# Seven block products instead of eight for three of eight pairs in an output projection

## The chip, the core and the metric

The kernel runs on one core of one Trainium2 chip. The metric is the device time of one execution in microseconds (us), median over runs. Five engines run their own instruction queues in order: PE (TensorE, matmuls), DVE (VectorE), ACT (ScalarE), POOL (GpSimd) and SP (SyncE, which here only issues transfers). They meet through semaphores. The profile names weight loads of PE apart, as PEld.

## The reference

Two layers of an encoder, 256 positions, width 2048, all in float32. Layer 0 mixes tokens with a gated MLP, layer 1 with latent attention (16 heads); each mixer and each feed-forward block ends in a residual sum and a layer norm. What the change touches is the last line of the attention and the norm behind it:

```
o = chunk_causal_attention(q_nope, q_rope, k_nope, k_rope, v)      # (1, 256, 16 heads, 128)
m = o.reshape(B, S, MLA_HEADS * V_DIM) @ w_out                     # (256 x 2048) @ (2048 x 2048)
x = layer_norm(ALPHA * x + m, ln_mix_g[i], ln_mix_b[i])
f = conv_ffn(x, ffn_w_up[i], ffn_conv_w[i], ffn_conv_b[i], ffn_w_down[i])
```

## The kernel before

**Float32 by parts.** Every float32 matrix is split into a rounded part (`wh`, made on ACT with a copy) and the rest (`wl`, made on DVE as raw minus rounded). One block product is then three matmuls of 512 columns: high by high, low by high, high by low (`prod_b`, line 366; every matmul is recorded at line 230, in `mm`).

**Weights.** A `Feed` walks one list of chunks, 1 MB each. SP loads a chunk into one of 3 `raw` buffers, ACT and DVE split it, PE uses it. The split parts stand in a pool with the tag `big`: 14 slots of 1 MB. A slot is given again when the last reader of its old content is done, so an ACT or DVE instruction that writes into a slot can wait for PE.

**The attention's output projection.** The 2048 columns of the result are done in two halves. For the first half (accumulators `mo0`) the matmuls are woven between the scores and the products of the heads. The second half (`mo1`) is a loop over eight chunks; a chunk is a pair of row blocks k (128 rows each) by 1024 columns. For each pair there are eight block products: two row blocks by two halves of positions (b) by two column blocks of 512 (f). The last three pairs (`SKEW`) are kept in `late`. `end_mo` adds them accumulator by accumulator, so that the accumulators finish one after the other, and `boundary` weaves the norm between: `piece` (add to the residual, statistics), `start` (mean and root), `scale` (normalize on DVE), `put` (four transposes on PE into `lnt`, scale and shift on ACT into `lny`, then the split into `xhl`, high part on ACT, low part on DVE). The first products of the feed-forward block (`upf`) read `xhl`.

**Seven products.** In the other large products of the kernel some pairs already use seven block products (Winograd's form of Strassen's method) by `Banks.seven`, `Feed._seven` and `combine`. Seven products need sums of the weights' blocks (`ts`, split into `th` and `tl`), sums of the activations' blocks (made by `turn` and `combine`), four further accumulators, and at the end `Banks.rest` and `Norm.fold`, eight DVE instructions that give back the four shared parts. A pair with eight products takes 2 slots of `big`, one with seven takes 5 (`ts`, `wh`, `wl`, `th`, `tl`).

**What sets the order.** The code is recorded by a tile framework. Its scheduler turns the recorded program into one fixed order per engine, by priorities and its own estimates of durations, with the needed semaphores. Lines such as `order(...)` and `keep_in_program_order` pin a few of them. On the chip each engine takes its instructions strictly in that order.

**Slots around the change.** During `mo1` the pool `big` holds `oT` (the heads' results, 4 slots) and the residual `res` (2 slots) throughout.

Of the kernel before, what the change touches and what calls it, by code (L numbers as in the profile page):

```python
# [8 lines left out]
F32 = mybir.dt.float32  # L9
F32R = mybir.dt.float32r  # L10
BF16 = mybir.dt.bfloat16
AF = mybir.ActivationFunctionType
ALU = mybir.AluOpType
AX = mybir.AxisListType

P = 128
S = 256
# [7 lines left out]
H = 16  # L25
# [19 lines left out]
SKEW = 3  # L45
# [5 lines left out]

U_PAIRS = [[0, 1, 5, 7, 2, 6, 3, 4]] + [[0, 1, 2, 5, 3, 7, 4, 6]] * 5
U_SEVEN = [(2, 3)] + [(2, 3, 4)] * 4 + [(2, 3)]

T1, T2 = 6, 5
SLOTS = {"big": 14, "raw": 3, "side": 6}
# [153 lines left out]
def trunk(ctx: ExitStack, tc: tile.TileContext, x, xT, gm_in, gm_wout, ffn_up, ffn_dn,  # L210
          ml_q, ml_kv, ml_b, ml_out, consts, w_sT, b_s, ropes, ln_rows, out):
    nc = tc.nc
# [3 lines left out]
    tp = ctx.enter_context(tc.tile_pool(name="tp", bufs=3))  # L216
# [6 lines left out]
    def slot(shape, name, dt=F32, tag="big"):  # L223
        return big.tile(shape, dt, tag=tag, name=name, bufs=SLOTS[tag])

    def bank(name):
        return ps.tile([P, 512], F32, tag="bank", name=name)

    def mm(o, l, r, start, stop):
        recent[0] = nc.tensor.matmul(o, l, r, start=start, stop=stop, skip_group_check=True)  # L230
        return recent[0]
# [12 lines left out]
    chunks, parked = [], []  # L244
# [4 lines left out]
    for g in range(6):  # L249
        for p in U_PAIRS[g]:  # L250
            i = 48 + 8 * g + p // 2
            w = gm_in[i : i + 5 : 4, :, p % 2 * 1024 : p % 2 * 1024 + 1024].rearrange("f p c -> p f c")
            chunks.append((w, 2048, "seven" if p in U_SEVEN[g] else "wide"))

# [15 lines left out]
    chunks += [(ml_q[i], 2048, "") for i in range(4)]  # L270
    chunks += [(ml_kv[i], 3 * KVR, "") for i in range(5)] + [(ml_kv[5, :, 0:KVR], KVR, "")]
    chunks += [(ml_b[i], 2048, "") for i in range(ml_b.shape[0])]
    chunks += [(ml_out[i], 2048, "") for i in range(ml_out.shape[0])]
    chunks += [(ffn_up[1, i], 2048, "") for i in range(n_up)]
    back(ffn_dn[1], NF_FF)

# [1 line left out]
    feed = Feed(nc, tc.keep_in_program_order, behind, order, big, dram, chunks)  # L278
# [9 lines left out]
    def turn(t, k1, k2):  # L288

        at = lambda k, b: k[:, b] if len(k.shape) == 3 else k[:, b * P : (b + 1) * P]  # L290
        tc.keep_in_program_order(nc.vector.tensor_tensor(t[:, 0], at(k1, 0), at(k1, 1), ALU.subtract))
        nc.vector.tensor_tensor(t[:, 1], at(k1, 1), at(k2, 1), ALU.subtract)
        nc.vector.tensor_tensor(t[:, 2], t[:, 1], at(k1, 0), ALU.subtract)
        nc.vector.tensor_tensor(t[:, 3], at(k2, 0), t[:, 2], ALU.add)

    def combine(name, o, k1, k2):


        t = tp.tile([P, 4, P], F32, tag="t2", name=f"xs{name}", bufs=T2)
        turn(t, k1, k2)  # L300
        o = o.rearrange("p (h s c) -> p h s c", h=2, s=4)
        nc.scalar.copy(o[:, 0], t)
        nc.vector.tensor_tensor(o[:, 1], t, o[:, 0].bitcast(F32), ALU.subtract)
        return [(o[:, 0, i], o[:, 1, i]) for i in (1, 2, 0, 3)]

    for j in range(4):
        t = slot([P, 4, S], f"xraw{j}", tag="side")
# [47 lines left out]
    def x_parts(xs, k, b):  # L355
        t = xs[k // 4]
        return (t[:, k % 4, b * P : (b + 1) * P], t[:, k % 4, S + b * P : S + (b + 1) * P])

    def prod_b(acc, parts, hi, lo, pieces, first, last):

        xh, xl = parts
        for f, (o, w) in enumerate(pieces):
            mm(acc[f][:, :w], xh, hi[:, o : o + w], first, False)
            mm(acc[f][:, :w], xl, hi[:, o : o + w], False, False)
            mm(acc[f][:, :w], xh, lo[:, o : o + w], False, last)
# [37 lines left out]
    OWN, DIRECT = ("p1", "q5", "p7", "p6"), ("q3", "p2", "e", "q4")  # L403
# [327 lines left out]
    halfp = [(0, 512), (512, 512)]  # L731
# [19 lines left out]
    for gi in range(6):  # L751

        acc = Banks(f"v{gi}", DIRECT if gi == 0 else OWN + DIRECT if gi % 2 else DIRECT + OWN)
        rest = (None,) * 4
        for c, p in enumerate(V_PAIRS[gi]):
            a = [[x_parts(xhl, 2 * p + j, b) for j in range(2)] for b in range(2)]
            got = feed.next()
# [19 lines left out]
            if c == 7 and gi == 5:  # L777
                wTg = []
                for i in range(4):
                    t = tp.tile([P, 2, P], F32, tag="t1", name=f"wT{i}", bufs=T1)  # L780
# [72 lines left out]
    def turned(g, tiles):  # L853

        for i, t in enumerate(tiles):
            src = v[g][:, i // 2, i % 2 * 512 : i % 2 * 512 + 512]
            for j in range(4):
                nc.tensor.transpose(t[:, j * P : (j + 1) * P], src[:, j * P : (j + 1) * P], ident)
            nc.scalar.copy(src, t)
# [7 lines left out]
    for g in range(6):  # L867
        direct, own = (ub[4:], ub[:4]) if g % 2 else (ub[:4], ub[4:])
        acc = Banks(f"u{g}", DIRECT + OWN, direct + own)
        for c, p in enumerate(U_PAIRS[g]):  # L870
            a = [[x_parts(xhl, 2 * p + j, b) for j in range(2)] for b in range(2)]
            got = feed.next()
            if p in U_SEVEN[g]:
                acc.seven(a, xc[p], *got, turned=512, across=True)
                if p == U_SEVEN[g][-1]:
                    rest = acc.rest()
# [21 lines left out]
    ln = Norm(0, {})  # L898
    acc, end = down(NF_GM, pT, "wo", ln, acts, tiles=ub, beside=lambda: turned(5, ub[4:]))
# [66 lines left out]
    ln, acc, end = ffn(0, ln, acc, end, False)  # L966
# [61 lines left out]
    acc = [[bank(f"mkv{b}_{f}") for f in range(2)] for b in range(2)]  # L1028
    for c in range(6):
        hi, lo = feed.next()  # L1030
        for j in range(3 if c < 5 else 1):
            k = 3 * c + j
# [9 lines left out]
    for b in range(2):  # L1042
# [3 lines left out]
        t = tp.tile([P, 4, ROPE], F32, tag="t1", name=f"kr2_{b}", bufs=T1)  # L1046
# [18 lines left out]
    acc = [[bank(f"qr{b}_{f}") for f in range(2)] for b in range(2)]  # L1065
    for c in range(2):
        hi, lo = feed.next()
        for j in range(2):
            k = 2 * c + j
# [52 lines left out]
    oT = []  # L1122
# [41 lines left out]
    def attend_b(h):  # L1164

        p = probs[h]
        pt = bank(f"pt{h}")
        for j in range(3):
            nc.tensor.transpose(pt[:, j * P : (j + 1) * P], p[:, j * P : (j + 1) * P], ident)  # L1169
        pts = tp.tile([P, 3 * P], F32, tag="t2", name=f"pts{h}", bufs=T2)  # L1170
        nc.scalar.copy(pts, pt[:, : 3 * P])
        probs[h] = pts

    def attend_c(h):
        if h % 4 == 0:
            oT.append(slot([P, 4, 512], f"oT{h // 4}", F32R))
        pts = probs.pop(h)
        o = bank(f"o{h}")
        c = slice(h * P, (h + 1) * P)
        mm(o[:, 0:S], vv[0][:, c], pts[:, 0:S], True, False)  # L1180
        mm(o[:, P:S], vv[1][:, c], pts[:, S : 3 * P], False, True)
        hi = oT[h // 4][:, h % 4, 0:S]
        nc.scalar.copy(hi, o[:, 0:S])
        nc.vector.tensor_tensor(oT[h // 4][:, h % 4, S : 2 * S], o[:, 0:S], hi.bitcast(F32), ALU.subtract)

    for hf in range(2):
        acc = [[bank(f"vv{hf}_{b}_{f}") for f in range(2)] for b in range(2)]
        for c in range(2):
            hi, lo = feed.next()
            for j in range(2):  # L1190

                k = 2 * c + j
# [7 lines left out]
        for b in range(2):  # L1200
            for f in range(2):
                c = slice(hf * 1024 + f * 512, hf * 1024 + (f + 1) * 512)
# [3 lines left out]
    ln = Norm(2, res)  # L1206
    acc = [[bank(f"mo0_{b}_{f}") for f in range(2)] for b in range(2)]
    LAG = 4
    attend_c(0)
    for t in range(3, H + LAG):  # L1210
        k = t - LAG
        if k >= 0:
            if k % 2 == 0:
                hi, lo = feed.next()
            w = slice((k % 2) * 1024, (k % 2) * 1024 + 1024)
        if 3 < t < H:
            attend_a(t)
        if k >= 0:
            prod_b(acc[0], x_parts(oT, k, 0), hi[:, w], lo[:, w], halfp, k == 0, k == KD - 1)
        if t < H + 2:  # L1220
            attend_c(t - 2)
        if k >= 0:
            prod_b(acc[1][:1], x_parts(oT, k, 1), hi[:, w], lo[:, w], halfp[:1], k == 0, k == KD - 1)
        if t - 1 < H:
            attend_b(t - 1)
        if k >= 0:
            prod_b(acc[1][1:], x_parts(oT, k, 1), hi[:, w], lo[:, w], halfp[1:], k == 0, k == KD - 1)
    ln.begin()
    ln.prep()
    for b in range(2):  # L1230
        for f in range(2):
            ln.piece(b, f, acc[b][f])
    acc = [[bank(f"mo1_{b}_{f}") for f in range(2)] for b in range(2)]
    late = []
    for c in range(8):
        left = 7 - c
        hi, lo = feed.next(splits=2 if left > 5 else 3, loads=2)
        for j in range(2):
            k = 2 * c + j
            w = slice(j * 1024, (j + 1) * 1024)  # L1240
            if left < SKEW:
                late.append((hi[:, w], lo[:, w], k))
                continue
            for b in range(2):
                prod_b(acc[b], x_parts(oT, k, b), hi[:, w], lo[:, w], halfp, k == 0, False)

    def end_mo(b, f):
        for hi, lo, k in late:
# [3 lines left out]
    ln, acc, end = ffn(1, ln, banks, end_mo, True)  # L1252
# [99 lines left out]
```

## Time and profile before

| what | value |
|---|---|
| time, median of 3 runs | 2465.73 us (2465.49 to 2466.3) |
| span of the profiled execution, first to last instruction | 2464.6 us |
| PE busy in the span | 2458.1 us, granted clock 1.000 |
| DVE busy | 2054.7 us |
| ACT busy | 1459.3 us |
| matmuls into `mo`, both halves: first and last start | 1637.3 and 1749.9 us |
| first product of the feed-forward block behind them, on PE | 1750.6 us |

The profiled execution has a span and no separate time of its own; the runs' times are whole device times, and their median lies 1.1 us over the span. Times of places below are us from the span's start. A busy PE in the profile is one with a matmul in its pipeline. Names lose their buffer numbers in the profile: `mo` is every accumulator of this projection.

### The profile page before, as it was taken

How to read it: one execution, taken by the hardware profiler on the slowest of the kernel's cores; microseconds unless marked ns; L12 is line 12 of the kernel's file. 1: busy time of each engine (PE TensorE's matmuls, PEld its weight loads, DVE VectorE, ACT ScalarE, POOL GpSimd, SP SyncE). 2: the span in 40 equal slices, each digit the busy share in tenths (PEclk: the TensorE clock that was granted, in tenths of full speed). 3: DMA queues.
4: the chain of work that ended last, by engine and by line, in shares of the span. 5: the costliest groups of instructions: out<-in, count | busy, mean ns of one | idle time of the engine just before them, and what ended most of it. 6: DMA issues, size and time to landing. Idle time of an engine off the chain costs nothing. (4 is left out here: it accounts for less than half of the span.)

```text
span 2464.6 us, 32483 instructions
## 1 busy us (share of the span) xinstructions
PE 2458.1 (100%) x12494; PEld 2091.3 (85%) x12494; DVE 2054.7 (83%) x2734; ACT 1459.3 (59%) x1967; POOL 104.2 (4%) x202
## 2 busy tenths in 40 slices
PE   9999999999999999999999999999999999999999
PEld 7888888888888888888888888988888888888887
DVE  7999999989897788778777997867598787878798
ACT  6666665566565666656554566665565665555453
POOL 0000000000000000000001000000000000000000
PEclk9999999999999999999999999999999999999999
DMA  7555666656665778778868885544478787777885
GB/s 291 202 208 205 226 204 202 205 188 205 222 212 198 241 282 314 300 279 300 322 218 318 301 301 182 184 170 156 172 269 309 275 305 304 295 265 278 299 324 201
DMA packets 116428, 611.94 MB, mean 248 GB/s; under 512 B 10648, under 2 KB 10912, under 8 KB 75184
## 3 DMA queue, kind: packets, MB, share of 16 engines
q1 hardware_dynamic: 90128, 462.47, 52.9%
q0 software_dynamic: 26144, 147.39, 15.8%
q8 instruction: 98, 1.61, 0.3%
q14 instruction: 58, 0.48, 0.1%
HBM read 544.75 MB, written 65.06 MB: 247 GB/s over the span
## 5 line engine op out<-in xcount | busy, mean ns | idle before, releaser
L128 DVE TENSOR_TENSOR wl<-raw,wh 128x1024 fp32r<-128x1024 f32 (+4 forms) x645 | 958.4, 1501 | 169.5 <-ACT wh L125 124.0
L125 ACT CAST wh<-raw 128x1024 fp32r<-128x1024 f32 (+4 forms) x645 | 809.0, 1278 | 356.8 <-PE up L230 80.7
L230 PE MATMUL up<-xhl,wh 128*128 128x512 f32 x2624 | 611.4, 390 | 0.0
L230 PEld LDWEIGHTS up<-xhl,wh 128*128 128x128 f32 x2624 | 487.4, 188 | 97.8
L230 PEld LDWEIGHTS up<-xhl,wl 128*128 128x128 f32 x2624 | 325.8, 192 | 6.4
L230 PE MATMUL up<-xhl,wl 128*128 128x256 f32 x2624 | 328.1, 283 | 0.0
L125 ACT CAST th<-ts 128x1536 fp32r<-128x1536 f32 (+1 forms) x138 | 142.5, 1052 | 110.9 <-DVE ts L135 80.3
L230 PE MATMUL ub<-wh,xhl 128*128 128x512 f32 x576 | 179.5, 393 | 0.0
L128 DVE TENSOR_TENSOR tl<-ts,th 128x1536 fp32r<-128x1536 f32 (+1 forms) x138 | 163.2, 1221 | 10.4 <-PE dn_p L230 3.4
L230 PEld LDWEIGHTS ub<-wh,xhl 128*128 128x128 f32 x576 | 108.1, 188 | 24.2 <-issue 1.9
L230 PE MATMUL ub<-wl,xhl 128*128 128x512 f32 x288 | 112.1, 389 | 0.0
L135 DVE TENSOR_TENSOR ts<-ts,raw 128x512 f32<-128x512 f32 x138 | 95.1, 689 | 1.4
L135 DVE TENSOR_TENSOR ts<-raw 128x1024 f32<-128x1024 f32 x69 | 84.3, 1221 | 6.1 <-PE ub L230 3.8
L230 PE MATMUL mo<-wh,oT 128*128 128x512 f32 x256 | 82.5, 401 | 0.0
L230 PE MATMUL v_q<-wh,xhl 128*128 128x512 f32 x224 | 70.7, 391 | 0.3 <-ACT wh L125 0.3
L230 PEld LDWEIGHTS ub<-wl,xhl 128*128 128x128 f32 x288 | 54.1, 188 | 11.3
L230 PE MATMUL v_p<-wh,xhl 128*128 128x512 f32 x192 | 59.9, 389 | 0.0
L230 PEld LDWEIGHTS mo<-wh,oT 128*128 128x128 f32 x256 | 45.5, 189 | 7.1
L230 PEld LDWEIGHTS v_q<-wh,xhl 128*128 128x128 f32 x224 | 42.0, 188 | 10.5 <-ACT wh L125 1.9
L230 PE MATMUL mo<-wl,oT 128*128 128x512 f32 x128 | 50.1, 391 | 0.0
L724 ACT ACTIVATE lny<-lnt,lncol 128x128 f32<-128x128 f32 x96 | 36.6, 472 | 15.6 <-PE lnt L720 15.5
L388 DVE TENSOR_TENSOR h_0a<-up,lo_0a 128x256 f32<-128x256 f32 x41 | 17.2, 421 | 33.0 <-ACT lo_0a L386 33.0
(1838 smaller groups left out, 4338.4 us busy)
## 6 DMA issues: line engine op xcount, KB each, us to landing
raw<-in_ffn_up_dram SPq DMA_DIRECT2D x172, 1024.0 KB, 7.0
raw<-in_gm_in_dram SPq DMA_DIRECT2D x93, 1024.0 KB, 5.3
raw<-in_ffn_dn_dram SPq DMA_DIRECT2D x68, 1024.0 KB, 7.2
raw<-in_gm_wout_dram SPq DMA_DIRECT2D x48, 1024.0 KB, 5.3
praw<-in_ffn_dn_dram POOLq DMA_DIRECT2D x16, 1024.0 KB, 13.9
keptth<-pth POOLq DMA_DIRECT2D x16, 1024.0 KB, 8.1
kepttl<-ptl POOLq DMA_DIRECT2D x16, 1024.0 KB, 8.8
fth<-keptth POOLq DMA_DIRECT2D x16, 1024.0 KB, 9.4
```

The lines of the kernel that those rows point to most:

```text
L125: cast = self.nc.scalar.copy(hi, raw)
L128: self.nc.vector.tensor_tensor(lo, raw, hi.bitcast(F32), ALU.subtract)
L135: add = lambda o, a, b: self.nc.vector.tensor_tensor(o, a, b, ALU.add)
L230: recent[0] = nc.tensor.matmul(o, l, r, start=start, stop=stop, skip_group_check=True)
L388: nc.vector.tensor_tensor(h, acc[:, 0:S], lo, ALU.add)
L724: nc.scalar.activation(y[:, j], t[:, j * P : (j + 1) * P], AF.Identity, bias=lncol[:, o : o + 1], scale=lncol[:, g : g + 1])
```

## The change

Pairs 2, 3 and 4 of the eight pairs of the second half take seven block products. The sums of activations for these pairs are made on DVE and ACT (`sum_heads`) at the end of the attention, behind the last scores. They stand in two further slots of `big` (`mos`) until the projection has used them. All eight accumulators are taken from the start; behind pair 4 `rest` and `fold` add the shared parts to the residual, and the four `piece` calls at the end become plain adds.

```diff
+MO_SEVEN = (2, 3, 4)
...
-    chunks += [(ml_out[i], 2048, "") for i in range(ml_out.shape[0])]
+    chunks += [(ml_out[i], 2048, "seven" if i - 8 in MO_SEVEN else "") for i in range(ml_out.shape[0])]
...
     attend_c(0)
+    mo_sums, mo_room = {}, []
+
+    def sum_heads(c):
+
+        if len(mo_sums) % 2 == 0:
+            mo_room.append(slot([P, 2, 8 * P], f"mos{c}", F32R))
+        x = oT[c // 2][:, 2 * (c % 2) : 2 * (c % 2) + 2]
+        raw = tp.tile([P, 2, S], F32, tag="t2", name=f"mor{c}", bufs=T2)
+        nc.vector.tensor_tensor(raw, x[:, :, 0:S].bitcast(F32), x[:, :, S : 2 * S].bitcast(F32), ALU.add)
+        mo_sums[c] = combine(f"mo{c}", mo_room[-1][:, len(mo_sums) % 2, :], raw[:, 0], raw[:, 1])
+
...
             attend_b(t - 1)
+        if 0 <= t - H - 1 < len(MO_SEVEN):
+            sum_heads(MO_SEVEN[t - H - 1])
...
-    acc = [[bank(f"mo1_{b}_{f}") for f in range(2)] for b in range(2)]
+    mo = Banks("mo1", DIRECT + OWN)
+    acc = [[mo.acc[DIRECT[2 * b + f]] for f in range(2)] for b in range(2)]
     late = []
     for c in range(8):
         left = 7 - c
-        hi, lo = feed.next(splits=2 if left > 5 else 3, loads=2)
-        for j in range(2):
-            k = 2 * c + j
-            w = slice(j * 1024, (j + 1) * 1024)
-            if left < SKEW:
-                late.append((hi[:, w], lo[:, w], k))
-                continue
-            for b in range(2):
-                prod_b(acc[b], x_parts(oT, k, b), hi[:, w], lo[:, w], halfp, k == 0, False)
+        got = feed.next(splits=2 if left > 5 else 3, loads=2)
+        if left < SKEW:
+            for j in range(2):
+                w = slice(j * 1024, (j + 1) * 1024)
+                late.append((got[0][:, w], got[1][:, w], 2 * c + j))
+            continue
+        a = [[x_parts(oT, 2 * c + j, b) for j in range(2)] for b in range(2)]
+        if c in MO_SEVEN:
+            mo.seven(a, mo_sums[c], *got)
+        else:
+            mo.eight(a, *got)
+        if c == MO_SEVEN[-1]:
+            for j, t in enumerate(mo.rest()):
+                ln.fold(j // 2, 2 + j % 2, t)
```

The change also makes the scheduler write another order around the end of the projection. The first place is PE's queue there. Before, with `mo_1_1` the last accumulator to finish and `lnt_0_0` the first transposes of the norm of the first 128 positions:

```order
L230 MATMUL mo_1_0_14431<-wl_14570,oT_14275 128x512
L230 MATMUL mo_1_1_14432<-wh_14503,oT_14074 128x512
L720 MATMUL lnt_0_0_14695<-ident,res_0_10982 128x128 x4
L230 MATMUL mo_1_1_14432<-wh_14503,oT_14074 128x512
L230 MATMUL mo_1_1_14432<-wl_14504,oT_14074 128x512
L230 MATMUL mo_1_1_14432<-wh_14503,oT_14074 128x512 x2
```

After, with `mo_q_14461` the last accumulator (the same block of the result as `mo_1_1`):

```order
L232 MATMUL mo_q_14461<-wh_14620,oT_14275 128x512 x2
L232 MATMUL mo_q_14461<-wl_14621,oT_14275 128x512
L722 MATMUL lnt_0_0_14757<-ident,res_0_10982 128x128 x4
L722 MATMUL lnt_0_1_14789<-ident,res_0_10982 128x128 x4
L232 MATMUL upf_0_14804<-wh_14663,xhl_0_14753 128x512
L722 MATMUL lnt_0_2_14818<-ident,res_1_11812 128x128 x4
L232 MATMUL upf_0_14804<-wh_14663,xhl_0_14753 128x512
```

The first transposes moved from one matmul into the last accumulator's products to behind all 18 of them.

The second place is DVE's queue at the same end. Before, where `res_0` and `res_1` are the residual's two column halves and `lnmv_0` is the mean and variance of the first 128 positions:

```order
L128 TENSOR_TENSOR wl_14610<-raw_14575,wh_14609 128x1024 x2
L666 SCALAR_TENSOR_TENSOR res_1_11812<-res_1_11812,mo_0_0_14429 128x512
L667 BN_STATS lnst_0_14419<-res_1_11812 128x6
L666 SCALAR_TENSOR_TENSOR res_1_11812<-res_1_11812,mo_0_1_14430 128x512
L667 BN_STATS lnst_0_14419<-res_1_11812 128x6
L672 BN_AGGR lnmv_0_14665<-lnst_0_14419 128x2
L351 RECIPROCAL lnrs_0_14669<-lnrs_0q 128x1
L679 TENSOR_SCALAR res_0_10982<-res_0_10982,lnmv_0_14665,lnrs_0_14669 128x512 x2
L666 SCALAR_TENSOR_TENSOR res_1_11812<-res_1_11812,mo_1_0_14431 128x512
```

After, from the third of the feed-forward block's weight splits on:

```order
L130 TENSOR_TENSOR wl_14680<-raw_14669,wh_14679 128x1024 x2
L666 TENSOR_TENSOR res_1_11812<-res_1_11812,mo_q_14458 128x512
L666 TENSOR_TENSOR res_1_11812<-res_1_11812,mo_p_14459 128x512
L669 BN_STATS lnst_0_14448<-res_1_11812 128x6 x2
L666 TENSOR_TENSOR res_1_11812<-res_1_11812,mo_e 128x512
L674 BN_AGGR lnmv_0_14727<-lnst_0_14448 128x2
L666 TENSOR_TENSOR res_1_11812<-res_1_11812,mo_q_14461 128x512
L669 BN_STATS lnst_1_14449<-res_1_11812 128x6 x2
L353 RECIPROCAL lnrs_0_14731<-lnrs_0q 128x1
L674 BN_AGGR lnmv_1_14843<-lnst_1_14449 128x2
L681 TENSOR_SCALAR res_0_10982<-res_0_10982,lnmv_0_14727,lnrs_0_14731 128x512 x2
```

The add of the last accumulator and the statistics of the second 128 positions now stand ahead of the first scaling of the first 128 positions, and three instead of two pairs of the feed-forward block's weights are split ahead of all that.

## The prediction

> **What bounds the kernel now.** I read the page first, then the busy times of the stage, then the timelines of PE and DVE around it.
>
> ```profile
> PE 2458.1 (100%) x12494; PEld 2091.3 (85%) x12494; DVE 2054.7 (83%) x2734; ACT 1459.3 (59%) x1967; POOL 104.2 (4%) x202
> PE 33%; DMA 1%; DVE 1%; issue 0%; ACT 0%; DVEq 0%; ACTq 0%
> ```
>
> PE is never idle for long and heads the chain of waits, so a matmul saved is time saved, as long as nothing makes PE wait. But DVE is busy for 83% of the span, and the change takes work from PE and gives work to DVE. So what counts is DVE's room in this stage. The busy times of two stretches of the second half (stretch and length, then busy us and number of instructions of PE, PEld, DVE, ACT and POOL, then granted clock and DMA):
>
> ```profile
> 1706.10:1717.00 10.90, 10.90 (x49) 9.03 (x49) 7.79 (x10) 4.01 (x4) 0.00 (x0) 1.00 0.52 191
> 1717.00:1750.00 33.00, 33.00 (x149) 27.29 (x149) 19.51 (x24) 15.00 (x19) 0.00 (x0) 1.00 0.50 187
> ```
>
> In the last 33 us DVE works 19.5 us; it has 13.5 us of room. Next, PE's rows there (start, duration, instruction):
>
> ```profile
> 1734.72 0.62 PE L230 MATMUL mo<-wh,oT 128*128 128x512 f32 x2
> 1735.40 0.62 PE L230 MATMUL mo<-wh,oT 128*128 128x512 f32 x2
> ...
> 1745.84 0.60 PE L720 MATMUL lnt<-ident,res 128*128 128x128 f32 x4
> ...
> 1749.94 0.39 PE L230 MATMUL mo<-wl,oT 128*128 128x512 f32 x1
> 1750.17 0.60 PE L720 MATMUL lnt<-ident,res 128*128 128x128 f32 x4
> ...
> 1751.62 0.50 PE L230 MATMUL upf<-wh,xhl 128*128 128x512 f32 x1
> ```
>
> Three matmuls, one block product, start 0.68 us after the three before: 0.227 us each. From the last matmul into `mo` at 1749.94, back over 192 of them and four transposes (about 0.4 us), the second half starts at about 1706.1, and its second pair ends at 1717.0 (48 x 0.227 = 10.9). The norm's first transposes run inside the last accumulator's products, and `upf` follows without a hole. DVE's rows show why:
>
> ```profile
> 1697.50 0.54 DVE L1161 TENSOR_SCALAR p<-p,mx 128x128 f32<-128x128 f32 x2
> ...
> 1744.00 1.00 DVE L679 TENSOR_SCALAR res<-res,lnmv,lnrs 128x512 f32<-128x512 f32 x2
> ...
> 1751.48 0.68 DVE L666 SCALAR_TENSOR_TENSOR res<-res,mo 128x512 f32<-128x512 f32 x1
> ```
>
> The first row is the last head's probabilities, needed below. DVE scales the first 128 positions at 1744.0, some 6 us before PE is done, and adds the last accumulator only at 1751.5.
>
> **What is removed.** Three pairs save one block product each: 9 matmuls x 0.227 = 2.0 us of PE, 0.08% of the time. That is the whole possible gain, and it is smaller than the 0.2% (4.9 us) that a measurement of this kernel can tell from no change.
>
> **What is added, and where it lies.** On DVE, all for float32. The same steps exist in the kernel's other products; what counts is the time until the next instruction starts, which is about 0.09 us less than the duration where rows follow each other. First a pair with seven products:
>
> ```profile
> 1363.77 1.22 DVE L135 TENSOR_TENSOR ts<-raw 128x1024 f32<-128x1024 f32 x1
> ...
> 1366.71 1.75 DVE L128 TENSOR_TENSOR wl<-raw,wh 128x1536 fp32r<-128x1536 f32 x1
> 1368.38 0.69 DVE L135 TENSOR_TENSOR ts<-ts,raw 128x512 f32<-128x512 f32 x1
> 1368.98 2.36 DVE L128 TENSOR_TENSOR tl<-ts,th 128x1536 fp32r<-128x1536 f32 x2
> 1371.25 0.69 DVE L488 TENSOR_TENSOR dn018wx<-act,dn018wx 128x512 fp32r<-128x512 f32 x1
> ```
>
> Then `rest` and `fold`, eight instructions from the first row to the second:
>
> ```profile
> 1375.52 0.69 DVE L451 TENSOR_TENSOR dn00u<-dn_p,dn00p 128x512 f32<-128x512 f32 x1
> ...
> 1380.32 1.23 DVE L128 TENSOR_TENSOR wl<-raw,wh 128x1024 fp32r<-128x1024 f32 x1
> ```
>
> Then two statistics and four splits in a row, in this stage:
>
> ```profile
> 1705.61 1.28 DVE L667 BATCH_NORM_STATS2 lnst<-res 128x6 f32<-128x512 f32 x2
> ...
> 1727.95 4.63 DVE L128 TENSOR_TENSOR wl<-raw,wh 128x1024 fp32r<-128x1024 f32 x4 [3.08 <-issue]
> ```
>
> A split of 1024 columns takes (4.63 - 1.22) / 3 = 1.135 us, a sum of 512 columns 0.60 (1368.38 to 1368.98), the split of 1536 columns 1.67, `tl` 2.27 and two statistics 1.2. A seven costs DVE 1.13 + 0.60 + 1.67 + 0.60 + 2.27 = 6.27 us against 2.27 for a plain pair. PE uses it up in 21 x 0.227 = 4.8 us. Three in a row put DVE behind.
>
> *The anchor.* `big` has 14 slots; `oT` holds 4, `res` 2 and the new sums 2, which leaves 6. Pairs 0 and 1 hold 4, so the first seven gets its fifth buffer, `tl`, only when PE is done with pair 1, at 1717.0. The sums themselves (three times two instructions of 0.60 and four short ones of 0.20, 6.0 us) lie before that. Pair 1's split (2.27) now stands behind them in DVE's queue instead of ahead of the last probabilities, so these move from 1697.5 to 1695.2. From there I count 0.5 (probabilities) + 0.3 (`oT`) + 6.0 (sums) + 0.3 (`oT`) + 2.3 (split of pair 1) + 4.8 (first half's adds and statistics) + 4.0 (first seven up to `tl`) = 18.2 us, done at about 1713.4. The sums cost nothing, with 3.6 us to spare; beyond that the rest moves with them.
>
> *DVE from 1717.0 to the first scaling*, in the order that its queue has after the change: `tl` of the first seven 2.27; two more sevens 12.54; the three late pairs 6.82; `rest` and `fold` 4.80 (1375.52 to 1380.32); three pairs of the feed-forward block 6.82; four adds and four statistics, 0.60 each, 4.80; mean, root and their waits about 0.5; the first scaling 0.5. Sum 39.1 us, so the first transposes can start at 1756.1. PE's own work from 1717.0 is 63 matmuls of sevens and 72 late ones, 135 x 0.227 = 30.7 us: done at 1747.7. PE waits about 8.4 us, because the queue has the scaling behind everything else. Waits of PE for a late `th` or `wl` before that only take from those 8.4.
>
> *The restart.* What follows a set of transposes is seen later in this boundary, on PE, ACT and DVE:
>
> ```profile
> 1759.94 0.60 PE L720 MATMUL lnt<-ident,res 128*128 128x128 f32 x4
> 1760.58 1.51 ACT L724 ACTIVATE lny<-lnt,lncol 128x128 f32<-128x128 f32 x4 [1.69 <-PE lnt L720]
> 1762.12 0.62 ACT L727 CAST xhl<-lny 128x512 fp32r<-128x512 f32 x1
> 1762.77 0.69 DVE L728 TENSOR_TENSOR xhl<-lny,xhl 128x512 fp32r<-128x512 f32 x1 [2.44 <-ACT xhl L727]
> ```
>
> From transposes to the low part of `xhl` 3.5 us, plus 0.4 for a fifth `lny` that stands ahead of the cast: 3.9. DVE's other seven scalings (0.46 each) fit within it. So the second matmul of `upf`, at 1751.62 before, comes at 1756.1 + 3.9 = 1760.0: 8.4 us later. The 2.0 saved is in this already. From there PE is the bound again as before, and nothing gives the delay back.
>
> *Hidden:* ACT gets three `mos` casts, three `th` and one copy; with 15.0 of 33 us used it stays off the path. SP issues the same transfers in the same order, later by what DVE is late with `raw`. The transfers of these weights land after 4.8 us (median):
>
> ```profile
> raw<-in_ffn_up_dram SPq DMA_DIRECT2D x10, 1024.0 KB, 4.8
> ```
>
> The last pair ahead of the norm can be loaded when DVE ends the late pairs; DVE then has 4.8 + 4.5 us of other work, which leaves 4.5 us for ACT's casts. If that cover went, DVE would wait and the end would move by as much.
>
> **The clock.** A hole of 8 us in PE does not occur in the middle of this trace. What an idle PE costs is seen at both ends of the span, in PE's first and last rows and in the busy times of the last 2.6 us:
>
> ```profile
> 1.31 4.45 PE L230 MATMUL warm<-idle 128*128 128x512 bf16 x10 [1.31 <-POOL idle L281]
> ```
>
> ```profile
> 2457.51 2.84 PE L230 MATMUL fin<-lng,dg 128*128 128x512 f32 x6 [0.27 <-DVE dg L701]
> ```
>
> ```profile
> 2462.00:2464.60 2.60, 0.00 (x0) 0.00 (x0) 0.00 (x0) 0.00 (x0) 0.00 (x0) 0.82 0.26 101
> ```
>
> Ten matmuls of 512 columns took 4.45 us at the start, 0.445 each, nearly twice 0.227: half speed, 2.2 us lost before full speed. After PE's last matmul (end at 2460.35) the granted clock averages 0.82 from 2462.0 to 2464.6; if it fell to 0.5 it did so at about 2463.7, 3.3 us into the idle time. A hole of 8 us should do the same, and PE then pays the start again: 2.2 us, the nearest row, with 0 and 4.4 (twice) as ends. The Trainium skill ("TensorE: Matmul & The Clock Gate", section "Part 1: The HAM clock gate") says that PE's clock halves after an idle window of about 3.4 us and comes back after about 3.4 us of sustained work. The trace's two ends agree (3.3 us and 4.45 us). By the page alone the loss would be an estimated 1.7 to 3.4 us, and the sum 2475.8 to 2477.5 us.
>
> **Sum.** 8.4 + 2.2 = 10.6 us on the profiled span of 2464.6 us, which lies 1.1 us below the median of the runs, 2465.73: 2476.3 us, 0.43% slower.
>
> **Rivals.**
> - *The same hole, and the clock stays.* For it: no hole in mid-program shows a fall. Against: the end of the span. 2465.7 + 8.4 = 2474.1.
> - *DVE keeps up; not slower.* Against it stand 39.1 us of DVE rows in 33 us. It needs some 6 us less, as if the fifth buffer came earlier or the rows ran closer. The queue order alone would still make PE wait from 1747.7 for one add, two statistics, root and a scaling (0.7 + 1.2 + 0.3 + 0.5 = 2.7), then 3.9 us to the second `upf` matmul, at 1754.3: +2.7, 2468.4, no change by the 0.2%.
> - *Only the saved products show.* If besides that the scaling were ready in time: 2465.7 - 2.0 = 2463.7, also no change. It decides for this once DVE is done by 1744 as before; the order on DVE, which puts the last accumulator's add first, excludes it nearly.
> - *Buffers starve the sevens.* With six slots for five buffers each, the later sevens wait for slots that PE frees late, and DVE stands still in between. For it: the first seven does so. Against: DVE is behind by then and finds the slots free. One further wait of a product's four groups, 4 x 0.68 = 2.7 us, with the clock: 2479.
>
> **How the numbers follow.** Hole and clock 0.62; hole alone 0.20; buffers 0.07; DVE keeps up 0.07; saved products alone 0.04. The likeliest gives 2476.3. Its own range is 2474 to 2479, from 1.5 us on DVE's chain either way and the clock's ends cut at about their middles. The range to hold 8 in 10 is 2471.5 to 2480: below, the hole alone with DVE's chain 2.6 us shorter; above, DVE's 1.5 us and the clock's upper end together. Slower by over 0.2% (above 2470.7) 0.89; within 0.2% 0.10; faster 0.01, since no mechanism gives more than 2.0 us.
>
> **What would show it.** DVE without idle time from about 1717 until the scaling; the first `lnt` behind the last `mo`, with PE idle for 7 to 9 us and then again for about 2 us ahead of `upf`, both released by DVE; a granted clock below 1 right behind, and matmuls of `upf` at about 0.43 us from start to start. Wrong would be: DVE idle in that stretch, PE's hole under 4 us, a clock of 1.00 throughout, or time lost elsewhere, in the attention's end (the sums) or in the first wait for a `th`.

## The result and the profile after

The changed kernel takes 2476.76 us (median of 4 runs, 2476.28 to 2477.01) against 2465.61 us for the kernel before (4 runs): 11.15 us more, ratio 1.0045 with a 95% interval of 1.0033 to 1.0057. The forecast was 2476.3. The profiled execution has a span of 2475.1 us.

The engines' busy times from the page, to be set beside those of before:

```profile
PE 2459.2 (99%) x12485; PEld 2092.8 (85%) x12485; DVE 2076.5 (84%) x2772; ACT 1467.1 (59%) x1974; POOL 104.2 (4%) x202
```

PE has nine matmuls fewer and is busy 1.1 us longer, a first sign of a slower clock. DVE has 21.8 us more. The same 33 us as before, from 1717 us on:

```profile
1717.00:1750.00 33.00, 30.76 (x133) 24.28 (x131) 32.93 (x35) 20.11 (x20) 0.00 (x0) 1.00 0.56 210
```

DVE went from 19.51 to 32.93 of 33 us: full. What PE waits for in this stage (us in total, times, longest), and below it what DVE waits for until the norm:

```profile
PE lnt L722 <- DVE res L681: 6.9, 1, 6.9
PE upf L232 <- ACT xhl L729: 1.7, 1, 1.7
PE mo_q L232 <- ACT th L127: 0.9, 1, 0.9
```

```profile
DVE tl L130 <- PE mo_q L232: 2.5, 1, 2.5
```

DVE waits once, for the fifth buffer of the first seven, and then not again until the scaling. Its timeline, from that `tl` to the scaling:

```profile
1716.38 2.36 DVE L130 TENSOR_TENSOR tl<-ts,th 128x1536 fp32r<-128x1536 f32 x2 [2.55 <-PE mo_q L232]
...
1753.04 0.64 DVE L666 TENSOR_TENSOR res<-res,mo_q 128x512 f32<-128x512 f32 x1
1753.58 1.29 DVE L669 BATCH_NORM_STATS2 lnst<-res 128x6 f32<-128x512 f32 x2
...
1755.08 1.85 DVE L681 TENSOR_SCALAR res<-res,lnmv,lnrs 128x512 f32<-128x512 f32 x4
```

PE's timeline at the same end:

```profile
1748.29 0.39 PE L232 MATMUL mo_q<-wl,oT 128*128 128x512 f32 x1
1755.62 1.97 PE L722 MATMUL lnt<-ident,res 128*128 128x128 f32 x8 [6.93 <-DVE res L681]
1759.25 0.79 PE L232 MATMUL upf<-wh,xhl 128*128 128x512 f32 x1 [1.66 <-ACT xhl L729]
...
1760.55 0.78 PE L232 MATMUL upf<-wh,xhl 128*128 128x512 f32 x1
1761.12 0.63 PE L232 MATMUL upf<-wl,xhl 128*128 128x512 f32 x1
1761.55 1.05 PE L232 MATMUL upf<-wh,xhl 128*128 128x512 f32 x2
1762.40 0.63 PE L232 MATMUL upf<-wl,xhl 128*128 128x512 f32 x1
```

The second matmul of `upf` is at 1760.55 (before 1751.62), 8.9 us late, and the matmuls behind it start 0.43 us apart (1761.12, 1761.55, then two until 1762.40): half clock. How far everything behind is shifted shows in the norm's 32 transposes (duration in ns, least, median and most; then first and last start), before and after:

```profile
L720 PE MATMUL lnt<-ident,res x32: 270/272/273, 1745.8 to 1770.0; 128*128 128x128 f32 x32
```

```profile
L722 PE MATMUL lnt<-ident,res x32: 270/273/477, 1755.6 to 1781.1; 128*128 128x128 f32 x32
```

The last one is 11.1 us late, about the 11.15 us of the runs. Over the two profiled executions as a whole the difference is 10.5 us (2475.1 against 2464.6): 0.6 us is given back far behind this place.

### The profile page after: what moved, and what is told of

It is laid out like the page before. It is cut to its first block, busy times and chain, and to the rows that moved or that the text cites. A ratio compares the mean times of both kernels' runs of the same rounds, so it can differ in the third digit from the quotient of the medians.

```text
span 2475.1 us, 32517 instructions
## 1 busy us (share of the span) xinstructions
PE 2459.2 (99%) x12485; PEld 2092.8 (85%) x12485; DVE 2076.5 (84%) x2772; ACT 1467.1 (59%) x1974; POOL 104.2 (4%) x202
## 5 line engine op out<-in xcount | busy, mean ns | idle before, releaser
L127 ACT CAST th<-ts 128x1536 fp32r<-128x1536 f32 (+1 forms) x144 | 148.7, 1050 | 118.3 <-DVE ts L137 89.0
L130 DVE TENSOR_TENSOR tl<-ts,th 128x1536 fp32r<-128x1536 f32 (+1 forms) x144 | 170.4, 1223 | 13.1 <-ACT th L127 3.6
L232 PE MATMUL upf<-wh,xhl 128*128 128x512 f32 x128 | 44.0, 417 | 1.7 <-ACT xhl L729 1.7
L154 DVE TENSOR_TENSOR praw<-praw 128x512 f32<-128x512 f32 x64 | 44.0, 688 | 0.5
L390 DVE TENSOR_TENSOR h_1a<-up,lo_1a 128x256 f32<-128x256 f32 x41 | 17.3, 421 | 31.9 <-ACT lo_1a L388 31.7
```

Of the source, the lines that this page charges most:

```text
L127: cast = self.nc.scalar.copy(hi, raw)
L130: self.nc.vector.tensor_tensor(lo, raw, hi.bitcast(F32), ALU.subtract)
L154: add = lambda o, a, b: pin(nc.vector.tensor_tensor(o, a, b, ALU.add))
L390: nc.vector.tensor_tensor(h, acc[:, 0:S], lo, ALU.add)
```

## The experiments

My theory: DVE, filled up by the sevens, reaches the scaling late, because that stands behind the backlog in its queue; PE idles, and then pays again with half clock. Rivals were the price of the sevens themselves (by number, or their sums or buffers), the order of DVE's queue by itself, the amount of DVE's work by itself, and a hole without any clock.

**Sums alone.** The sums of activations are made; all pairs take eight products.

```
-    chunks += [(ml_out[i], 2048, "seven" if i - 8 in MO_SEVEN else "") ...]
+    chunks += [(ml_out[i], 2048, "") ...]
...
+            mo.eight(a, *got)          # for every pair; no seven, rest or fold
```

> The sums of activations are made at the same place, but all pairs have eight products and nothing reads the sums (no rest, no fold). Theory: the sums lie in DVE's spare time behind the last scores and cost nothing: 2465.6 us, within 0.3. Rival (the sums and the displaced split of pair 1 hold up the last heads or the first products of the second half): slower by 1 to 6 us, the time of their DVE instructions.

Measured: 2465.25 us (before 2465.36), ratio 0.9999 (0.9990 to 1.0008). The sums cost nothing.

**Two sevens, in pairs 2 and 3, and in pairs 3 and 4.**

```
-MO_SEVEN = (2, 3, 4)
+MO_SEVEN = (2, 3)        # the other kernel: (3, 4)
```

> Pairs 2 and 3 with seven products, pair 4 with eight. Theory (DVE's backlog at the end, and the place of the scaling in its queue): DVE has 6.27 - 2.27 = 4.0 us less, rest and fold come a pair earlier, and in the order of this kernel the first scaling of the first 128 positions stands ahead of the last accumulator's add again, with the fourth feed-forward pair behind it. PE finds the transposes ready, no hole, clock 1.00; 6 products saved x 0.227 = 1.4 us: 2464.2 to 2465.0 us. Rival (each seven costs here, by its sums, its five buffers or its own waits, and three cost 11.1 us): two thirds, 2473 us. Rival (rest and fold with their four further accumulators cost once, whatever the number): 2470 us or more.

> Pairs 3 and 4 with seven products: the same number of instructions on each engine as with pairs 2 and 3, one pair later. In this kernel's order rest and fold come one pair later, and the first scaling stands behind the last accumulator's add and its statistics, as in the changed kernel. Theory (order and backlog): PE waits 2 to 3.5 us ahead of the first transposes, with the restart +4 us against before; if the clock falls again (2.5 us of idle time were enough in the changed kernel) another 1.5 to 2.2: 2469.5 to 2471.8 us. Rival (the cost goes by the number of sevens): the same time as with pairs 2 and 3.

Measured: 2465.02 us with (2, 3), ratio 0.9997 (0.9988 to 1.0006), and 2472.24 us with (3, 4), ratio 1.0027 (1.0016 to 1.0037). The two do the same work. Their engine rows, (2, 3) first:

```profile
PE 2456.6 (100%) x12488; PEld 2091.1 (85%) x12488; DVE 2071.1 (84%) x2762; ACT 1464.9 (59%) x1972; POOL 104.2 (4%) x202
```

```profile
PE 2459.3 (100%) x12488; PEld 2093.6 (85%) x12488; DVE 2070.9 (84%) x2762; ACT 1465.0 (59%) x1972; POOL 104.2 (4%) x202
```

DVE's and PE's rows with (2, 3): the scaling starts at 1746.06, and the first transposes run inside the last accumulator's products.

```profile
1746.06 1.01 DVE L681 TENSOR_SCALAR res<-res,lnmv,lnrs 128x512 f32<-128x512 f32 x2
1746.66 0.66 PE L722 MATMUL lnt<-ident,res 128*128 128x128 f32 x4
```

With (3, 4), `rest` and `fold` come a pair later, the scaling stands behind the last add, and PE waits:

```profile
1751.04 1.85 DVE L681 TENSOR_SCALAR res<-res,lnmv,lnrs 128x512 f32<-128x512 f32 x4
1751.57 1.97 PE L722 MATMUL lnt<-ident,res 128*128 128x128 f32 x8 [3.32 <-DVE res L681]
```

Both rivals of a price by seven or by `rest` fall: equal counts, 7.2 us apart. With (3, 4) the loss was 0.4 us over my range. With (2, 3) it was at my range's upper end. Of the 1.4 us that it saves in products 0.3 arrived, which these runs cannot tell from nothing; its trace shows two short waits of PE there, 0.4 us for a `wl` and 0.2 us ahead of `upf`. It is the best of the versions run, and not measurably faster than the kernel before.

**DVE's work without its place in the queue.**

```
+        if zero:                              # tl of pairs 2, 3, 4 only
+            self.nc.gpsimd.memset(lo.bitcast(F32), 0.0)
+            return cast
         self.nc.vector.tensor_tensor(lo, raw, hi.bitcast(F32), ALU.subtract)
```

> The low parts tl of the three sums of weights are set to zero by POOL, which is idle, in place of DVE's three pairs of instructions: that part of the computation is left out; PE's products are all made. DVE has 6.8 us less to do, while the add of the last accumulator and the statistics behind it still stand ahead of the first scaling in its queue. Theory (backlog and place in the queue, each with a share): with the backlog gone, DVE still waits for PE's last products ahead of its queue, does one add, two statistics, root and a scaling; counting its queue row by row, PE waits 3 to 4.5 us instead of 6.9, and the clock still falls: 2470.5 to 2472.5 us. Rival (the amount of DVE's work alone makes the hole): 6.8 us less leave next to nothing of it, the clock stays: 2464 to 2466 us. Rival (the place in the queue alone): 2476.8 us, unchanged.

Measured: 2471.97 us, ratio 1.0025 (1.0015 to 1.0035).

```profile
PE lnt L725 <- DVE res L684: 4.1, 1, 4.1
```

With 6.8 us less on DVE the first scaling came 4.0 us sooner (1751.04 against 1755.08), and PE still waits 4.1 us: less work alone did not close the hole. In this kernel's order the last of the splits, the last add and its statistics still stand ahead of the scaling. But 2.3 of the 6.8 us went into further waits of DVE for PE and ACT (4.8 us before the norm, against 2.5), and PE itself was done 1.1 us sooner (its last product for `mo_q` starts at 1747.17 instead of 1748.29). So this run does not separate amount and place cleanly.

**The place without the work.** The norm's DVE steps pinned in the order of the code.

```
+            pin = tc.keep_in_program_order if self.idx == 2 and (b, f) in self.folded else lambda ins: ins
-                nc.vector.tensor_tensor(r, r, acc, ALU.add)
+                pin(nc.vector.tensor_tensor(r, r, acc, ALU.add))     # likewise bn_stats and the scaling
```

> The same work, but on DVE the adds, statistics and scalings of this norm are pinned in the order in which the code has them: first scaling of the first 128 positions ahead of the third accumulator's add. Three pairs of the feed-forward block are still split ahead of all. Theory (backlog with place in the queue): the first transposes come 1.7 to 2 us sooner than in the changed kernel (two adds and two statistics less ahead of the scaling, two waits more for ACT's root), PE still waits about 5 us, the clock still falls, and what is pushed behind comes late instead: the low parts of xhl and the fourth feed-forward pair hold up upf for about 2 us in all. 2475.5 to 2477.5 us, no better than the changed kernel's 2476.8. Rival (the place in the queue is what costs): the hole goes down to nothing or little, 2464 to 2470 us.

Measured: 2477.04 us, ratio 1.0046 (1.0033 to 1.0059), as the changed kernel. PE's waits:

```profile
PE lnt L724 <- DVE res L683: 5.4, 1, 5.4
PE upf L232 <- ACT xhl L731: 1.7, 1, 1.7
PE upf L232 <- ACT wh L127: 0.7, 1, 0.7
PE upf L232 <- DVE wl L130: 0.5, 1, 0.5
PE upf L232 <- DVE xhl L732: 0.2, 1, 0.2
```

The hole shrank by 1.5 us, and what was pushed behind the scaling is missed later, 1.4 us in three waits. This order moves the loss about; it does not remove it. It leaves the three pairs of the feed-forward block where they were, ahead of all; the next run moves those.

**One pair of the feed-forward weights ahead instead of three.**

```
-        got = feed.next(splits=2 if left > 5 else 3, loads=2)
+        got = feed.next(splits=2 if left > 5 else min(3, left + 1), loads=2)
```

> The same three sevens, but the loop splits at most one pair of the feed-forward block's weights ahead of the norm; the others are split behind its first steps. DVE's queue has two pairs, 4.5 us, less ahead of the scaling. Theory (backlog): PE's first wait goes from 6.9 to 2.4 to 3 us, the restart's 1.7 to 2.2 stay; the pairs that are split later are waited for only a little, since PE needs them one after the other: about 5.5 us later than before without the clock, 1.5 to 2.5 more with it (gaps of 2 us were enough for a short fall): 2472 to 2473.5 us. Rival (the pairs pushed behind are missed one for one): 2476 us or more. Rival (any removal of DVE's work ahead of the scaling closes the hole for good): 2465 to 2468 us.

Measured: 2472.27 us, ratio 1.0026 (1.0016 to 1.0036).

```profile
PE lnt L722 <- DVE res L681: 2.7, 1, 2.7
```

Of the edits that keep the whole computation with three sevens and add nothing, this one won most, 4.5 us. DVE has the same work; two pairs, 4.5 us of it, go from ahead of the scaling to a place where PE does not wait for them.

**The sums in other slots.**

```
-            mo_room.append(slot([P, 2, 8 * P], f"mos{c}", F32R))
+            mo_room.append(slot([P, 2, 8 * P], f"mos{c}", F32R, "side"))
```

> The sums of activations stand in two slots of the pool with the tag side, which is free in this stage, in place of two of big. The first seven then has its five buffers as soon as it wants them: tl no longer waits for PE's end of pair 1. Theory (DVE's total work in this stage, with no spare time left): DVE only wins the 2.5 us that it idled ahead of that tl, since everything behind is DVE's own work; the first scaling comes some 2.4 us sooner, PE's wait for th (0.9) goes too: 2474.0 to 2474.8 us. Rival (the slot is the anchor of the loss, as the prediction wrote it: what DVE does ahead of the scaling starts with PE's end of pair 1): the chain could start up to 3 us sooner and more where later waits go as well, 2472 us or less. Rival (slots have no part in it): 2476.8 us.

Measured: 2474.78 us, ratio 1.0037 (1.0023 to 1.0050), at the upper end of the theory's range. The `tl` of the first seven no longer waits, and the scaling starts 2.66 us sooner:

```profile
1713.24 2.35 DVE L130 TENSOR_TENSOR tl<-ts,th 128x1536 fp32r<-128x1536 f32 x2
...
1752.42 1.92 DVE L681 TENSOR_SCALAR res<-res,lnmv,lnrs 128x512 f32<-128x512 f32 x4
```

So the fifth buffer did set where DVE's chain began. Freeing it won 2.7 us at the scaling and 2.0 us of the time, about the 2.5 us that DVE had idled for it and no more.

**The clock by itself.** PE is kept busy where it idled, with products whose results are not used. DVE's and ACT's orders stay word for word.

```
...
+            for _ in range(N):     # behind the last accumulator's last product
+                order(mm(t, oT[3][:, 0, 0:P], oT[3][:, 0, :], True, True), ins)
...                                 # further lines pin what follows on PE behind them
```

With 28 such matmuls ahead of the first transposes:

> The changed kernel with 28 further matmuls of 512 columns on PE (28 x 0.227 = 6.4 us, results not used) between the last accumulator's last product and the first transposes, where PE was idle for 6.93 us. DVE's and ACT's orders are unchanged. Theory (hole plus clock): the hole's 8.9 us up to the second matmul of upf stays, since DVE still ends the scaling when it did; the granted clock stays at 1.00, and the other 2.2 us go: 2474.5 us, transposes and upf at full speed. Rival (the hole alone makes the loss, and the slow clock hides beside other waits): 2476.8 us as before. If filling delays something (the accumulator bank, the transposes), up to 0.5 us more.

Measured: 2475.93 us (2475.53 to 2476.91), between the two. These runs overlap with those of the changed kernel, so the times alone do not tell the two apart; the trace does. The clock's row of a stretch (columns as in the stretches above) shows that the gap ahead of `upf`, which stayed empty, let the clock fall after all.

```profile
PE upf L233 <- ACT xhl L735: 2.1, 1, 2.1
PE lnt L726 <- DVE res L685: 0.6, 1, 0.6
```

```profile
1755.88:1759.29 3.41, 1.35 (x9) 1.08 (x10) 3.37 (x9) 2.67 (x8) 0.00 (x0) 1.00 0.01 2
1759.29:1762.70 3.41, 3.41 (x13) 2.90 (x13) 1.20 (x2) 2.89 (x9) 0.00 (x0) 0.50 0.00 0
```

With 8 more in that second gap:

> As the kernel with 28 filling matmuls, and with 8 more (8 x 0.227 = 1.8 us) between the second transposes and the first product of upf, where PE there idled for 2.06 us and the clock fell for a short time. DVE's and ACT's orders are those of the changed kernel. Theory (hole plus clock): the granted clock stays at 1.00 throughout; transposes, their evictions and the second product of upf end as early as DVE's scaling at 1755.5 lets them: second product of upf at about 1759.8 (8.2 us later than before), and from there no loss: 2473.4 to 2474.2 us, so that the clock's whole share is 2.6 to 3.4 us of the 11.1. Rival (the clock's share is only the 0.9 us that the first filling saved): 2475.9 us.

Measured: 2473.83 us (2473.34 to 2474.48), ratio 1.0033 (1.0020 to 1.0045), inside the expected range, clock 1.000 throughout.

```profile
1755.35 1.11 PE L732 MATMUL lnt<-ident,res 128*128 128x128 f32 x8 [0.56 <-DVE res L691]
...
1759.55 0.48 PE L233 MATMUL upf<-wh,xhl 128*128 128x512 f32 x1
```

```profile
L732 PE MATMUL lnt<-ident,res x32: 270/272/328, 1755.4 to 1777.8; 128*128 128x128 f32 x32
```

The last transpose is 7.8 us later than before with the clock held, against 11.1: 3.3 us in the trace. By the runs it is 11.15 - 8.05 = 3.1 us (the intervals of the two ratios overlap; the runs themselves lie apart), and by the two profiled spans 2475.1 - 2472.7 = 2.4 us. So the hole costs about 8 us and the clock about 3.

With the first hole left empty and 4 matmuls in the second gap alone:

> The first hole of 6.9 us stays empty; 4 filling matmuls (at half clock about 0.43 us each, 1.7 us) stand only between the second transposes and the first product of upf. DVE's and ACT's orders are those of the changed kernel. In six kernels the granted clock stayed low for 3.41, 6.8, 10.2 (three times) and 13.65 us, that is 1, 2, 3 and 4 times 3.41; it came back after a stretch of 3.41 us in which PE was busy throughout, and did not after stretches with PE busy for 50 to 63%. Theory (the clock is judged by stretches of 3.41 us): the stretch with the restart, which had the gap of 1.66 us, is now full, and the clock comes back one stretch sooner, at about 1761.4 instead of 1764.8: low for 10.2 us; some 7 matmuls more at full speed, 1.5 to 1.7 us won: 2475.0 to 2475.6 us. Rival (the clock comes back after a fixed amount of PE's work or after a fixed time): low for 13.65 us or some value between, 2476.8 us or slower by what the filling delays.

Measured: 2474.41 us (2473.94 to 2475.14), ratio 1.0037 (1.0024 to 1.0049): 0.6 us better than my range. PE's 6.9 us hole is there as in the changed kernel, and the clock was low for two stretches, not the three I expected:

```profile
1745.41:1748.83 3.42, 2.66 (x12) 1.88 (x10) 3.42 (x4) 3.04 (x3) 0.00 (x0) 1.00 0.76 283
1748.83:1752.24 3.41, 0.00 (x0) 0.00 (x0) 3.41 (x6) 0.00 (x0) 0.00 (x0) 1.00 1.03 399
1752.24:1755.65 3.41, 0.64 (x3) 0.64 (x4) 3.41 (x10) 0.59 (x2) 0.00 (x0) 0.50 0.58 240
1755.65:1759.08 3.43, 3.43 (x12) 2.54 (x11) 3.12 (x8) 2.85 (x8) 0.00 (x0) 0.50 0.00 0
1759.08:1762.49 3.41, 3.41 (x20) 2.80 (x19) 0.92 (x2) 3.21 (x8) 0.00 (x0) 1.00 0.02 5
```

The filled stretch brought the clock back at once. But the stretches lie elsewhere in this execution: the hole began just ahead of a stretch, and the fall came 4.2 us into it (1748.07 to 1752.24). A fixed time at low clock falls with this, and a fixed amount of PE's work too: PE was busy for 4.07 us at half clock here and, by the rows in the last section, for 7.50 us in the changed kernel. How much of the gain is the filling and how much the place of the stretches, this run alone does not tell. In the kernel with the scaling first the fall also came late, 4.4 us into the hole, the second gap stayed empty, and the clock was low for three stretches.

## Why the prediction was right

The mechanism held; two sizes were off and partly cancelled, and one of the signs named in advance was not the one seen.

- *What is removed, and DVE as the engine that counts.* Right. Two sevens in pairs 2 and 3, which DVE can carry, lose nothing; the three lose 11 us.
- *The sums.* Put at no cost with 3.6 us to spare. Alone they cost nothing. The new `tl` shows the spare time: DVE idled 2.55 us ahead of it.
- *The anchor at 1717.0.* PE's end of pair 1 did release that `tl`, at 1716.38, 0.6 us sooner than counted.
- *DVE's 39.1 us.* From 1716.38 until PE's transposes, which the first scaling releases, at 1755.62 it took 39.2 us without idle time. The queue order that the sum followed was the one that ran.
- *PE done at 1747.7.* It was 1748.7, mainly from the wait of 0.9 us for a `th`. As the text said, that only took from the hole. With the transposes 0.5 us sooner than counted (1755.62 for 1756.1) it was 6.9 instead of 8.4 us.
- *The restart, 3.9 us.* At full clock it was 4.2 us (1755.35 to 1759.55 in the kernel with both gaps filled), in the changed kernel 4.9.
- *The second gap.* It came, 1.66 us for "about 2". But the forecast had it released by DVE, and the profile has it released by ACT's cast of `xhl` (L729); PE has no wait for DVE's low part there.
- *The clock, 2.2 us.* The mechanism was right, the size too small: 3.1 us. The step that failed is taking the price of the first ten matmuls of the span as the nearest row. There PE is fed without a break. (That these ten ran at half clock is read from their durations, 0.63 us each as in `upf` at half clock; the profile's clock record begins only behind them, and its views print 1.00 there. Their 4.45 us, which the forecast counted as agreeing with about 3.4, are longer than one of the stretches of 3.41 us seen here.) Here the transposes, a gap of 1.66 us and single matmuls come first, and the clock stayed at half for 13.65 us. My range of 0 to 4.4 held it. The estimate by the Trainium skill ("TensorE: Matmul & The Clock Gate", section "Part 1: The HAM clock gate"), 1.7 to 3.4 us, held it as well.
- *Sum.* 8.4 + 2.2 = 10.6 forecast; 8.05 + 3.1 = 11.15 measured, where the 3.1 is the difference of the two measured losses. The hole was put 0.35 us too high and the clock 0.9 us too low; that these two misses cancel in part is luck.
- *Rivals.* "Hole alone" fell with the filled kernels. "DVE keeps up" describes the kernel with pairs 2 and 3, not this one. "Buffers starve the sevens" had one wait, the counted one; freeing it gave 2.0 us.

What I had not weighed enough: I wrote that PE waits "because the queue has the scaling behind everything else". Pinning the scaling ahead gave nothing, and taking away 6.8 us of DVE's work left 4.1 us of the hole. Taking two pairs of splits from ahead of the scaling, with all the work kept, won 4.5 us. I read this as backlog and place in the queue acting together. How they combine is argued, not shown: no run has both the scaling first and the splits behind it.

## What to carry to other kernels

Before trading matmuls for vector work, add up the vector engine's rows between its last idle time and the instruction that PE waits for next; if they exceed PE's work in that stretch, PE idles for the difference and again during the restart (here 6.9 and 1.7 us), and the products saved give back only their own time (here 2.0 us). Two sevens cost nothing or 7 us here, by which pairs took them. Price a hole in PE with the clock too, by counting how many stretches of 3.41 us pass until one is full of PE work again.

## What the runs showed of the hardware

In these runs the granted clock changed in steps of 3.41 us. In the eight kernels with a fall it was low for 3.41 (28 matmuls in the first hole), 6.8 (one pair ahead; second gap filled), 10.2 (pairs 3 and 4; no `tl`; scaling first) and 13.65 us (the changed kernel; sums in other slots): whole multiples of 3.41, to within 0.05 us. The changed kernel, cut at those borders:

```profile
1747.72:1751.13 3.41, 0.96 (x5) 0.46 (x3) 3.41 (x5) 1.34 (x2) 0.00 (x0) 1.00 1.00 418
1751.13:1754.54 3.41, 0.00 (x0) 0.00 (x0) 3.41 (x8) 0.29 (x1) 0.00 (x0) 0.50 0.98 411
1754.54:1757.95 3.41, 1.97 (x8) 1.57 (x8) 3.37 (x10) 1.41 (x5) 0.00 (x0) 0.50 0.01 5
1757.95:1761.37 3.42, 2.12 (x7) 1.85 (x8) 1.69 (x4) 2.74 (x9) 0.00 (x0) 0.50 0.02 5
1761.37:1764.78 3.41, 3.41 (x9) 2.64 (x9) 1.39 (x2) 2.20 (x6) 0.00 (x0) 0.50 0.00 0
1764.78:1768.19 3.41, 3.41 (x18) 2.81 (x18) 0.24 (x1) 2.41 (x6) 0.00 (x0) 1.00 0.00 0
```

The fall follows a stretch in which PE was busy for 0.96 of 3.41 us (28%), and 1.35 us (40%) was still too little, in the first filled kernel. No fall followed 2.66 us (78%) in the kernel with the second gap filled. In all eight kernels the clock came back behind the first stretch that was full; 1.97 and 2.12 us (58 and 62%, at half clock) were not enough, nor were 2.75 us (81%) in the kernel with the sums in other slots:

```profile
1755.99:1759.40 3.41, 2.75 (x9) 2.28 (x10) 1.14 (x3) 2.74 (x8) 0.00 (x0) 0.50 0.02 5
1759.40:1762.82 3.41, 3.41 (x10) 2.53 (x9) 1.31 (x2) 1.57 (x4) 0.00 (x0) 0.50 0.00 0
1762.82:1766.23 3.41, 3.41 (x18) 2.87 (x17) 0.59 (x1) 2.75 (x6) 0.00 (x0) 1.00 0.00 0
```

An idle time of 2.1 us, with 0.6 us of idle time ahead of it, was enough for a fall, in the first filled kernel. The hole of 6.9 us was followed by four stretches at half clock in the changed kernel and by two in the kernel with the second gap filled; there the hole also lay elsewhere among the stretches, and the two causes are not separated. The fall came 2.4 us into the hole in the one and 4.2 us into it in the other. The Trainium skill ("TensorE: Matmul & The Clock Gate", section "Part 1: The HAM clock gate") describes a free-running window of 3413 ns; the traces agree with its length (3.41 us) and, by these 2.4 and 4.2 us, with its running free. Where the page speaks of an idle window, these runs show that a window with PE busy for 40% of it is enough.
